# One core, hybrid attention block: the last merge gates computed as twelve seven-product groups, sums of x made earlier, norm weight folded into scales

## The chip, the core and the metric

The kernel runs on one core of a Trainium2 chip. The metric is the device time of one execution in microseconds (us). Below, PE is TensorE's matmul queue, DVE VectorE, ACT ScalarE, POOL GpSimd, and SP the queue of SyncE that issues nearly all DMAs.

## The reference

x is 2048 x 1024 (float32). What matters here:

```python
h = rms_norm(x, norm_gain[layer])
proj = h @ w_in[layer]
qa, ka, va, qb, kb, vb, ga, gb, mg = jnp.split(proj, split_idx, axis=-1)
...
br_a = ya @ w_branch_a[layer]
br_b = yb @ w_branch_b[layer]
gates = jax.nn.sigmoid(mg.reshape(bsz, S, N_BRANCHES, D) + b_merge[layer])
merged = gates[:, :, 0] * br_a + gates[:, :, 1] * br_b
x = x + merged @ w_out[layer]
```

`ya` and `yb` are the outputs of two attention mixers, each times a SiLU path. `mg` is 2048 x 2048: for each of the eight 128-wide chunks of the model dimension, a gate column block for branch 0 and one for branch 1.

## The kernel before, in words

**Precision.** Every operand of a large product is split into two float16 halves, high and low, and three products are added: high x high, high x low, low x high. x, normalised but without the norm weight, stays transposed in XH and XL (128 partitions, 8 chunks of 128 channels, 2048 tokens, and 256 wrapped around). The norm weight `gn` is multiplied into the weights on POOL (`w_gain`, line 196) before their squares are summed on ACT for a power-of-two scale (`w_square`, `w_sum`, `w_pow`), and before they are split: the high half on ACT (`w_hi`, line 249), the low half on DVE (`w_lo`, line 255). All this is done in four pieces of two channels each, 768 elements per partition for a unit.

**Units' stage.** There are 14 units of attention heads, eight slots each, 112 slots. A slot projects two blocks of 128 tokens, 2 x 24 products of 384 columns (line 710), into one of two banks called `pj`. ACT reads q and k (line 727) and the high half of v (line 736), DVE the low half of v (line 742), and only then may PE fill that bank again. Norms, transposes by DMA, logits, softmax and values of earlier blocks follow in the same slots on the other engines. Some slots carry a fill: one gate chunk for 512 tokens, 24 products of 512 columns (`FILLS`, line 115), into `pj` as well; c = 2 to 7 are chunks of the SiLU paths, c = 8 and 9 are the merge gates of chunk 6, c = 10 and 11 those of chunk 7. Chunk 3 follows after the last unit (`mg_step`). Nothing is scheduled by the compiler: every step of the other engines is pushed with a planned time in slots (`at`) and comes out between PE's products in that order (`until`), so each engine's queue is fixed by hand.

**Tail.** Then come, with times in us from its start, the merge gates of chunks 1, 5, 0, 4, 2 (`DCS`, line 46), n = 0 to 4. Tokens of q = 1 and q = 3 (quarters of 512) use `gate_pair` (line 1393), 2 x 24 products. Tokens of q = 0 and q = 2 with both branches form a 2 x 2 block product over halves of the channels, and `gate_group` (line 1490) computes it with seven block products of 12 in place of eight: four plain blocks of x, four sums of them (S1 to S4, `x_sums`, line 1436), and sums of weights (T1, T2, T3, N4, `w_sums`, line 1461). Each of the seven goes to a bank of its own and is combined on ACT, DVE and POOL. The sums of x for this token pair are made in the tail, four chains of 16 steps, and kept in the left-over part of `wt`, the tile that holds the blocks of the output weights.

```python
steps = ((whole, v1, c, 1024), (whole, v2, c + 4, 1024), (V.tensor_tensor, v2, v1, v2, OP.add), (hi, v2, 0),
```

`prep` (line 1413) loads and splits a chunk's weights, `b_load` and `b_blocks` make blocks of the output weights (j = 0 to 3, all in the tail), and some 45 tiny DVE instructions (lines 1299 to 1327) make scales at the tail's start. The tail is followed by the branch stage (`branch_pair`) and the output products (`group`), both on PE throughout.

Of the kernel before, what the change touches and what calls it, by code (L numbers as in the profile page):

```python
# [32 lines left out]
S = 2048  # L33
# [12 lines left out]
DCS = (3, 1, 5, 0, 4, 2)  # L46
# [38 lines left out]
G_LATE = {11: 0.3}  # L85
# [29 lines left out]
FILLS = ((2, None, (2, 2, 4, 5)), (3, 0, (8, 9, 10, 12)), (4, 1, (17, 18, 20, 21)), (5, 2, (24, 25, 26, 28)), (6, 3, (32, 35, 37, 38)), (7, 4, (40, 41, 42, 44)), (9, 6, (57, 59, 60, 61)), (10, 7, (64, 65, 66, 68)), (11, 10, (88, 89, 90, 92)), (8, 13, (116, 116, 118, 118)))  # L115
# [9 lines left out]
def block_kernel(tc, x, w_units, w_gate, w_mrg, w_brn, w_out, w_bra, gain, qkg, sink, bias_a, bias_b, b_merge, out):  # L125
# [15 lines left out]
    ubuf = us.tile([128, 168], F32, name="ubuf")  # L141
# [36 lines left out]
    wtiles = {}  # L178
# [17 lines left out]
    def w_gain(u, i):  # L196
        gains(wtiles[u][0], 2 * i, 384 if u < NU else 256)
# [112 lines left out]
    mgd = {k: dr.tile([128, S], F32, name=f"mgd{k}") for k in range(16)}  # L310
    ymx = us.tile([128, 32], F32, name="ymx")
# [885 lines left out]

    un, nxt = None, 0.0
# [77 lines left out]
    ygs, ypool = {}, [(fg, 6, "fg")]  # L1276
# [38 lines left out]
    V.tensor_tensor(bnd[:], invb[0][:], invb[1][:], OP.add)
    V.tensor_scalar(bnd[:], bnd[:], 2.0 ** 31, None, OP.mult)
    s_m, i_m = pow2(bnd[:], "m")

    inv_m, rmx = ucol(), ucol()
    V.tensor_tensor(inv_m[:], invb[0][:], invb[1][:], OP.max)  # L1320
    V.reciprocal(rmx[:], inv_m[:])
    for c in range(8):
        V.tensor_scalar(rho[c][:], rho[c][:], invb[c // 4][:], rmx[:], OP.mult, OP.mult)
    V.tensor_scalar(inv_m[:], inv_m[:], s_m[:], 0.125, OP.mult, OP.mult)
    i_o, so4 = ucol(), ucol()
    V.tensor_scalar(i_o[:], i_m[:], io[:], 16.0, OP.mult, OP.mult)
    V.tensor_scalar(so4[:], so[:], 0.25, None, OP.mult)
# [65 lines left out]
    def gate_pair(n, q):  # L1393
        dc, u = DCS[n + 1], NU + 1 + n
        if n not in ims:
            assert ("w", u) in done
            ims[n] = ucol()
            V.tensor_scalar(ims[n][:], wtiles[u][2][:], 0.5 / SX, None, OP.mult)
        for k in range(2):
            ps = bank()  # L1400
            g = fg.tile([128, 512], F32, name="fg", bufs=6)

            def tanh(ps=ps, g=g, k=k):
                A.activation(g[:], ps[:], AF.Tanh, bias=bmh[:, 8 * k + dc:8 * k + dc + 1], scale=ims[n][:])

            def store(g=g, k=k):
                nc.sync.dma_start(out=mgd[2 * dc + k][:, 512 * q:512 * q + 512], in_=g[:])

            e = job(5.2, tproj_list(ps, *wtiles[u][3:5], 128 * k, q))
            at(e + T_GATE[0], tanh)  # L1410
            at(e + T_GATE[4], store)

# [12 lines left out]
    def xsum(i, c):  # L1425
# [429 lines left out]
```

## Time and profile before

| | us |
|---|---|
| median of three runs | 1909.31 |
| lowest and highest run | 1909.27, 1910.56 |
| profiled execution, first to last instruction (span) | 1907.4 |
| units' stage (first to last projection) | 69.1 to 1328.7 |
| chunk 3's gates and c = 8 | 1328.7 to 1398.9 |
| tail (gates) | 1398.9 to 1593.3 |
| branch stage, output products | to 1759.2, to 1907.4 |

The page gives each engine's busy time and the chain of work that ended last; other views of the same execution give the instructions in order of time, groups of them by line and shape (count, busy time, mean of one, idle time before them and who ended it), each engine's waits, and busy time by stretch. PE's instructions are pipelined: the length shown for one is longer than the distance to the next.

### The profile page before, as it was taken

Reading aid. Unit: us, or ns where it says so; the run is one execution under the profiler, and the core shown is the slowest. Engines: PE = TensorE matmul, PEld = TensorE weight load, DVE = VectorE, ACT = ScalarE, POOL = GpSimd, SP = SyncE. Lnnn points to the kernel's source line nnn. Section 1 sums busy time; section 2 is a strip of 40 time slices with the busy share of each in tenths; the row PEclk is TensorE's granted clock in tenths of the full one; section 3 lists DMA queues with packets and bytes.
Section 4 is the critical chain, followed back from the end, with each engine's and each line's share of the span. In section 5 each row is a group of like instructions: output and inputs, shape, how many; then the busy total and the mean of one; then the engine's idle time right before and its main releaser. Section 6 shows DMA issues by size and latency. Waiting matters only on the chain.

```text
span 1907.4 us, 39286 instructions
## 1 busy us (share of the span) xinstructions
PE 1898.5 (100%) x13578; PEld 1190.9 (62%) x13578; DVE 1355.2 (71%) x3522; ACT 1119.2 (59%) x2496; POOL 848.7 (44%) x1848
## 2 busy tenths in 40 slices
PE   8999999999999999999999999999999999999999
PEld 6566776677766688566787667876544444444444
DVE  7578887887767877577776877868686667867312
ACT  8468776777666776566776767666444645423100
POOL 4334454344545655446555666555412211223443
PEclk9999999999999999999999999999999999999999
DMA  8459987798868697578768788666822246887853
GB/s 292 122 106 182 195 171 149 150 195 157 189 108 195 132 186 135 123 149 183 165 128 156 159 181 145 131 125 124 189 73 100 105 155 221 236 253 246 282 209 137
DMA packets 624585, 316.56 MB, mean 166 GB/s; under 512 B 492928, under 2 KB 562176, under 8 KB 623104
## 3 DMA queue, kind: packets, MB, share of 16 engines
q1 hardware_dynamic: 605952, 305.39, 69.3%
q10 hardware_dynamic: 18432, 8.66, 1.8%
q8 instruction: 106, 1.74, 0.4%
q14 instruction: 95, 0.78, 0.1%
HBM read 129.91 MB, written 65.27 MB: 102 GB/s over the span
## 4 chain that ended last, share of the span: by engine, by line
PE 95%; DVE 2%; POOL 1%; issue 1%; ACT 1%; DMA 0%; SPq 0%; DVEq 0%; POOLq 0%; ACTq 0%
PE pj L710 44%; PE pj L334 16%; PE fps L334 11%; PE fps L1722 6%; PE s L880 5%; PE pv L929 5%; PE fps L1517 3%; PE pj L1722 2%; PE pj L610 2%; PE pj L1517 1%; ACT jk L482 0%; DMA xt<-in_x_dram 0%; PE pt L1001 0%; DVE XL L531 0%; DVE pr L895 0%
## 5 line engine op out<-in xcount | busy, mean ns | idle before, releaser
L710 PE MATMUL pj<-wh,XL 128*128 128x384 f16 x1792 | 586.1, 327 | 0.0
L710 PE MATMUL pj<-wl,XH 128*128 128x384 f16 x1792 | 584.7, 326 | 0.0
L710 PE MATMUL pj<-wh,XH 128*128 128x384 f16 x1792 | 584.4, 326 | 0.2 <-DVE vt L742 0.2
L710 PEld LDWEIGHTS <-XH 128*128 128x128 f16 x3584 | 410.4, 116 | 151.0 <-issue 0.9
L895 DVE CUSTOM_DVE_ANT_0 pr<-s,b,ubuf 128x256 f32<-128x256 f32 (+3 forms) x512 | 219.0, 465 | 77.3 <-PE s L880 75.3
L710 PEld LDWEIGHTS <-XL 128*128 128x128 f16 x1792 | 207.8, 116 | 69.1
L912 DVE SCALAR_TENSOR_TENSOR p<-pr,p 128x512 f16<-128x512 f32 (+2 forms) x256 | 190.2, 743 | 19.1 <-ACT p L908 19.0
L787 POOL COPY spl<-spl 128x256 f16<-128x256 f16 (+1 forms) x224 | 88.6, 425 | 183.3 <-DVE spl L782 181.9
L727 ACT ACTIVATE rw<-pj 128x256 f32<-128x256 f32 (+1 forms) x224 | 86.8, 387 | 134.4 <-PE pj L710 123.2
L908 ACT ACTIVATE p<-pr 128x512 f16<-128x512 f32 (+2 forms) x256 | 159.2, 622 | 6.4 <-issue 0.3
L334 PEld LDWEIGHTS <-wh 128*128 128x128 f16 x960 | 93.7, 98 | 110.5
L880 PE MATMUL s<-kq 128*128 128x256 f16 (+3 forms) x1168 | 147.8, 254 | 0.3 <-DMA kq<-spl 0.3
L929 PEld LDWEIGHTS <-pt 128*128 128x128 f16 x3024 | 125.4, 97 | 34.8
L287 POOL TENSOR_TENSOR rs_t<-rs_y 128x8 f32<-128x8 f32 (+1 forms) x112 | 41.2, 368 | 231.3 <-DVE rs_y L279 182.7
L772 POOL TENSOR_TENSOR rw<-rw,g 128x256 f32<-128x256 f32 (+1 forms) x112 | 91.4, 816 | 109.5 <-DVE rw L766 73.1
L194 POOL TENSOR_TENSOR wraw<-wraw,gn 128x768 f32<-128x768 f32 (+1 forms) x80 | 112.5, 1412 | 56.0 <-DMA wraw<-in_w_mrg_dram 43.5
L929 PE MATMUL pv<-vt,pt 128*128 128x65 f16 (+1 forms) x3024 | 132.7, 192 | 0.0
L880 PEld LDWEIGHTS <-kq 128*128 128x128 f16 x1184 | 101.7, 98 | 42.3 <-DMA kq<-spl 0.8
L766 DVE TENSOR_TENSOR rw<-rw,qr 128x512 f32<-128x512 f32 (+1 forms) x112 | 102.6, 916 | 32.0 <-POOL qr L296 31.1
L742 DVE SCALAR_TENSOR_TENSOR vt<-pj,vt 128x128 f16<-128x128 f32 (+1 forms) x224 | 62.1, 277 | 88.6 <-ACT vt L736 87.9
L334 PE MATMUL pj<-XH,gh 128*128 128x512 f16 x320 | 121.3, 379 | 0.0
L334 PE MATMUL pj<-XH,gl 128*128 128x512 f16 x320 | 121.2, 379 | 0.0
(281 smaller groups left out, 3797.9 us busy)
## 6 DMA issues: line engine op xcount, KB each, us to landing
wraw<-in_w_units_dram SPq DMA_DIRECT2D x56, 384.0 KB, 4.4
mtd<-mm SPq DMA_DIRECT2D x56, 256.0 KB, 3.7
M<-mtd SPq DMA_DIRECT2D x8, 1792.0 KB, 9.8
mgd<-fg SPq DMA_DIRECT2D x39, 256.0 KB, 2.1
zd<-z ACTq DMA_DIRECT2D x128, 66.0 KB, 2.5
zz<-zd SPq DMA_DIRECT2D x64, 132.0 KB, 2.8
xt<-in_x_dram SPq DMA_DIRECT2D x16, 512.0 KB, 9.3
gtd<-yo SPq DMA_DIRECT2D x32, 256.0 KB, 2.9
```

What stands on the lines that cost most here:

```text
L194: G.tensor_tensor(v, v, gn[:, c0:c0 + 2].unsqueeze(2).to_broadcast([128, 2, n]), OP.mult)
L334: out.append(lambda w=w, xx=xx, ch=ch, i=i: T.matmul(ps[:], lhsT=w[:, ch, c0:c0 + 128], rhs=xx[:, ch, ts], start=(i == 0), stop=(i == n - 1)))
L710: out.append(lambda lhs=lhs, rhs=rhs, ch=ch, k=k: T.matmul(ps[:, :384], lhsT=lhs[:, ch, :], rhs=rhs[:, ch, :], start=(k == 0), stop=(k == ...
L766: V.tensor_tensor(q, q, self.rr[:, :n].unsqueeze(2).to_broadcast([128, n, HD]), OP.mult)
L772: G.tensor_tensor(k, k, GT[un.br][:].unsqueeze(1).unsqueeze(1).to_broadcast([128, 2, un.nk, HD]), OP.mult)
L787: G.tensor_copy(sp[:, i, nh:, :, :], sp[:, i, nq:nh, ::-1, :])
L880: T.matmul(self.sv[j][:, o:o + k1 - k0], lhsT=q[:, h, qo:qo + 128], rhs=kt[:, un.nq + kh + v * un.nk, k0:k1], start=(v == 0), stop=(v == 1))
L895: V.tensor_tensor_reduce(out=self.pv[:, j, self.p0:self.p0 + W], in0=self.sv[j], in1=un.bias[:, self.h0 + j, self.b0:self.b0 + W], scale=I ...
L908: A.activation(self.sp[:, :128 * n], self.pr, AF.Copy, scale=PSC)
L912: V.scalar_tensor_tensor(self.sp[:, 128 * n:], self.pr, PSC, self.sp[:, :128 * n], OP.mult, OP.subtract)
L929: T.matmul(self.po[:, j, :w], lhsT=p[:, n * j + s, :], rhs=un.v[key][:, vh, c0:c0 + w], start=(k == 0 and s == 0), stop=(k == 2 and s == n ...
L1722: mm.append(lambda ch=ch, k=k, w=w, i=i: T.matmul(ps[:, :cols.stop - cols.start], lhsT=m[:, a, ch, k, :], rhs=wt[w][:, b, ch, cols], start ...
```

## The change

- `DCS` gets chunk 7 and `NG` is 6; the fills c = 10 and 11 go, and c = 6, 9 and 7 take over slots 40 to 44, 64 to 68 and 88 to 92.
- All six chunks are computed by `gate_group` for both token pairs (p = 0: q = 0 and 2, p = 1: q = 1 and 3), the two groups of a chunk step by step in turn. `gate_pair` goes. Products whose results are only added go into the same bank without a start, three banks per group in place of seven; the additions on POOL go.
- The sums of x are made for both pairs in the units' stage, in eight chains of 16 steps spread over slots 5 to 16, 19 to 33, 44 to 59, 68 to 83 and 93 to 104, each stored to DRAM. The tail loads them back in 52 DMAs, S2 and S3 at its start.
- For units, POOL's multiplication by the norm weight goes. ACT squares each channel with the weight as its scale, and the splits use a scale per channel, so each piece is two instructions of 384.
- The tiny scale instructions move 60 us into the tail, one at a time; the output weights' blocks use the sums' scratch tile, and block j = 3 moves into the branch stage.

```diff
-DCS = (3, 1, 5, 0, 4, 2)
+DCS = (3, 1, 5, 0, 4, 2, 7)
+NG = 6
...
+X_SUM = ((5, 16), (19, 33), (44, 59), (68, 83), (93, 104)), 0.2
...
+T_R = (60.0, 1.2)
+T_X = ((1, 0.0), (2, 2.0), (0, 14.0), (3, 22.0))
...
     def w_gain(u, i):
+        if u < NU:
+            return
         gains(wtiles[u][0], 2 * i, 384 if u < NU else 256)
...
+        if u < NU:
+            for c in (2 * i, 2 * i + 1):
+                A.activation(wtiles[u][2][:, c, :], raw[:, c, :], AF.Square, scale=gn[:, c:c + 1], accum_out=wtiles[u][3][:, c:c + 1])
+            return
...
+        if u < NU:
+            wgs[u] = sm.tile([128, NCH], F32, name="gs")
+            V.tensor_scalar(wgs[u][:], gn[:], s[:], None, OP.mult)
...
+        if u < NU:
+            for c in (2 * i, 2 * i + 1):
+                V.scalar_tensor_tensor(wl[:, c, :], raw[:, c, :], wgs[u][:, c:c + 1], wh[:, c, :], OP.mult, OP.subtract)
...
+        def whole(o, ch, tok):
+            tok += 512 * p
+            V.tensor_tensor(o, XH[:, ch, tok:tok + 512], XL[:, ch, tok:tok + 512], OP.add)
+
+        def hi(v, i):
+            A.activation(sx[:, 4 + i % 3, 0], v, AF.Copy, scale=X_SC[i])
+
+        def lo(v, i):
+            V.scalar_tensor_tensor(sx[:, 4 + i % 3, 1], v, X_SC[i], sx[:, 4 + i % 3, 0], OP.mult, OP.subtract)
+            at(now[0] + X_SUM[1], store, i)
+
+        def store(i):
+            nc.sync.dma_start(out=xsd[p][:, i, c], in_=sx[:, 4 + i % 3])
...
+    times = spread(128, X_SUM[0])
+    for k in range(8):
+        x_sums(times[16 * k:16 * k + 16], k // 4, k % 4)
...
+        steps = [("x", A11, B11, one), ("y", S2, T2, lambda ps: plus("c", "a", ps)), ("x", A12, B21, two),
+                 ("y", S3, T3, lambda ps: plus("d", "a", ps)), ("z", S1, T1, done_("d", "d", 1, 2)),
+                 ("y", A22, N4, done_("a", "a", 0, 2)), ("z", S4, B22, done_("c", "c", 1, 0))]
+        if n == 0:
+            steps[1:3] = steps[2:0:-1]
+        for z, x, bl, f in steps:
+            first = z not in banks
+            if first:
+                banks[z] = bank()
+            ps = banks[z]
+            at(job(2.6, products(ps, x, bl, first)) + T_GATE[0], f, ps)
             yield
...
+    for i, d in T_X:
+        for p in range(2):
+            at(t + d + .01 * p, xs_load, p, i)
+    at(t + T_R[0], run, tail_scales())
...
-    group0 = gate_group(0)
-    for n, q in ((0, 1), (0, 3), (group0, 2), (1, 1), (1, 3), (group0, 5), (gate_group(1), 7), (2, 1), (2, 3),
-                 (gate_group(2), 7), (gate_group(3), 7), (gate_group(4), 7), (3, 1), (3, 3), (4, 1), (4, 3)):
-        if isinstance(n, int):
-            gate_pair(n, q)
-        else:
-            for _ in range(q):
-                next(n)
+    for n in range(NG):
+        for _ in zip(gate_group(n, 0), gate_group(n, 1)):
+            pass
```

## Rows read from the trace of the kernel before

**Rows 1.** The page: span, granted clock by slice, chain by engine.

```profile
span 1907.4 us, 39286 instructions
...
PEclk9999999999999999999999999999999999999999
...
PE 95%; DVE 2%; POOL 1%; issue 1%; ACT 1%; DMA 0%; SPq 0%; DVEq 0%; POOLq 0%; ACTq 0%
```

**Rows 2.** PE's waits, 69 to 1400 us: total, times, longest.

```profile
PE pj L710 <- DVE vt L742: 0.2, 1, 0.2
```

**Rows 3.** The chain in order of time, tail: start, length, count.

```profile
1445.76 7.77 PE fps L1517 x36
...
1476.87 19.64 PE fps L334 x91
```

**Rows 4.** By stretch: length; PE, PEld, DVE, ACT, POOL busy (instructions); clock; DMA share; GB/s.

```profile
129.10:280.00 150.90, 150.90 (x1440) 104.39 (x1436) 128.50 (x332) 114.37 (x248) 68.02 (x161) 1.00 0.96 179
318.20:508.80 190.60, 190.60 (x1734) 138.35 (x1733) 155.15 (x425) 140.01 (x311) 78.49 (x196) 1.00 0.85 169
640.80:786.70 145.90, 145.90 (x1182) 112.36 (x1180) 108.43 (x322) 101.56 (x255) 84.29 (x220) 1.00 0.76 154
901.60:1042.10 140.50, 140.50 (x1155) 109.94 (x1154) 105.59 (x311) 98.40 (x250) 79.25 (x214) 1.00 0.78 154
1156.20:1256.50 100.30, 100.30 (x848) 84.28 (x847) 77.38 (x242) 67.02 (x171) 55.43 (x151) 1.00 0.73 137
1016.30:1088.40 72.10, 72.10 (x593) 46.93 (x591) 57.38 (x168) 50.53 (x134) 44.80 (x118) 1.00 0.77 153
...
1398.90:1593.30 194.40, 194.37 (x905) 88.11 (x903) 132.08 (x224) 102.49 (x172) 33.32 (x26) 1.00 0.36 121
1593.30:1759.20 165.90, 165.90 (x770) 75.25 (x769) 128.31 (x188) 60.49 (x96) 43.67 (x31) 1.00 0.80 247
```

**Rows 5.** Groups by line and shape, tail: the sums' steps today.

```profile
L1449 DVE SCALAR_TENSOR_TENSOR wt<-Y,wt 128x512 f16<-128x512 f32 x16 | 11.8, 736 | 0.1
L1445 ACT ACTIVATE wt<-Y 128x512 f16<-128x512 f32 x16 | 10.1, 629 | 15.3 <-DVE Y L434 15.1
```

**Rows 6.** Groups by line and shape: splits of 768 (units), of 384 (tail).

```profile
L259 DVE SCALAR_TENSOR_TENSOR wl<-wraw,ubuf,wh 128x768 f16<-128x768 f32 x53 | 56.9, 1073 | 9.9 <-ACT wh L253 9.0
L253 ACT ACTIVATE wh<-wraw,ubuf 128x768 f16<-128x768 f32 x52 | 48.1, 925 | 0.0
L1381 DVE SCALAR_TENSOR_TENSOR wl<-wraw,ubuf,wh 128x384 f16<-128x384 f32 x8 | 4.8, 614 | 4.0 <-ACT wh L1380 4.0
L1380 ACT ACTIVATE wh<-wraw,ubuf 128x384 f16<-128x384 f32 x8 | 4.4, 602 | 0.0
```

**Rows 7.** L766: min/median/max ns, then its group; in order of time, one collision.

```profile
L766 DVE TENSOR_TENSOR rw<-rw,qr x112: 678/693/2071, 83.0 to 1338.1; 128x512 f32<-128x512 f32 x96, 128x640 f32<-128x640 f32 x16
...
L766 DVE TENSOR_TENSOR rw<-rw,qr 128x512 f32<-128x512 f32 x95 | 84.7, 892 | 28.9 <-POOL qr L296 28.1
...
298.01 2.07 DVE L766 TENSOR_TENSOR rw<-rw,qr 128x640 f32<-128x640 f32 x1 [0.94 <-POOL qr L296]
...
297.93 1.47 POOL L194 TENSOR_TENSOR wraw<-wraw,gn 128x768 f32<-128x768 f32 x1
```

**Rows 8.** PE in order of time at one refilled bank: start, length.

```profile
1093.02 0.32 PE L710 MATMUL pj<-wh,XH 128*128 128x384 f16 x1 [0.23 <-DVE vt L742]
```

**Rows 9.** DVE in order of time: the first unit's last low half.

```profile
68.66 1.01 DVE L259 SCALAR_TENSOR_TENSOR wl<-wraw,ubuf,wh 128x768 f16<-128x768 f32 x1
```

**Rows 10.** DMA: throughput by slice, landing of a store, SP's issues around the tail's start.

```profile
GB/s 292 122 106 182 195 171 149 150 195 157 189 108 195 132 186 135 123 149 183 165 128 156 159 181 145 131 125 124 189 73 100 105 155 221 236 253 246 282 209 137
...
mgd<-fg SPq DMA_DIRECT2D x39, 256.0 KB, 2.1
...
1394.62 5.53 SPq L417 DMA_DIRECT2D mgd<-yo  x2
1404.76 1.41 SPq L189 DMA_DIRECT2D wraw<-in_w_mrg_dram  x3
```

More of the change, by code (lines that the diff above doesn't have):

```diff
@@ L310, in block_kernel @@
     mgd = {k: dr.tile([128, S], F32, name=f"mgd{k}") for k in range(16)}
+    xsd = [dr.tile([128, 4, 4, 2, 512], F16, name=f"xsd{p}") for p in range(2)]
+    sx = us.tile([128, 7, 2, 512], F16, name="sx")
     ymx = us.tile([128, 32], F32, name="ymx")
@@ L1315, in block_kernel @@
[L1315 to L1325, printed above, removed]
@@ L1334, in block_kernel, with run @@
+    def run(steps):
+        if next(steps, run) is not run:
+            at(now[0] + T_R[1], run, steps)
     A11, A12, A22, S1, S2, S3, S4 = range(7)
@@ L1391, in block_kernel @@
     ims = {}
[L1393 to L1411, printed above, removed]
     def prep(t, u):
@@ L1517, in products @@
                     mm.append(lambda ch=ch, k=k, w=w, i=i: T.matmul(
-                        ps[:], lhsT=weight(bl, ch)[w], rhs=xblock(x, ch)[k], start=(i == 0), stop=(i == 11)))
+                        ps[:], lhsT=weight(bl, ch)[w], rhs=xblock(x, ch, p)[k], start=(first and i == 0), stop=(i == 11), skip_group_check=not first))
             return mm
-        def copy(o, ps, scale):
-            A.activation(o, whole(ps), AF.Copy, scale=scale)
-        def plus(o, ps, v, scale):
-            V.scalar_tensor_tensor(o, whole(ps), scale, v, OP.mult, OP.add)
@@ L1527, in add @@
-        def add(o, x, y):
-            G.tensor_tensor(o, x, y, OP.add)
-        def gate(o, v, k, q, late):
-            at(now[0] + late, lambda: A.activation(o, v, AF.Tanh, bias=bmh[:, 8 * k + dc:8 * k + dc + 1], scale=ims[n][:]))
-            at(now[0] + late + T_S[6], lambda: nc.sync.dma_start(out=whole(mgd[2 * dc + k][:, 512 * q:512 * q + 512]), in_=o))
-        def two(ps):
-            d = tile_()
-            plus(d, ps, a, 1.0)
-            gate(d, d, 0, 0, T_S[8])
-        steps = ((A11, B11, lambda ps: copy(a, ps, 1.0)), (A12, B21, two), (S1, T1, lambda ps: copy(b, ps, 16.0)),
-                 (S2, T2, lambda ps: (plus(c, ps, a, 16.0), add(a, b, c))),
-                 (S3, T3, lambda ps: (plus(c, ps, c, 16.0), add(b, b, c), gate(b, b, 1, 2, T_S[7]))),
-                 (S4, B22, lambda ps: (plus(a, ps, a, 4.0), gate(a, a, 1, 0, T_S[8]))),
-                 (A22, N4, lambda ps: (plus(c, ps, c, 4.0), gate(c, c, 0, 2, T_S[8]))))
@@ L1544, in gate_group, with gate @@
-        for k, (x, bl, f) in enumerate(steps):
-            if k == 0 and n:
-                a = tile_()
-            if k == 2:
-                b, c = tile_(), tile_()
-            ps = bank()
-            at(job(2.6, products(ps, x, bl)) + T_GATE[0], f, ps)
-            yield
-    t = clock[0]
+        def gate(o, v, k, q, late, first=False):
+            at(now[0] + late, lambda: A.activation(o, v, AF.Tanh, bias=bmh[:, 8 * k + dc:8 * k + dc + 1], scale=ims[n][0 if first else 1][:]))
+            at(now[0] + late + T_S[6], lambda: nc.sync.dma_start(out=mgd[2 * dc + k][:, 512 * (q + p):512 * (q + p) + 512], in_=o))
@@ new lines, in gate_group, with one, plus, done_ @@
+        v = {}
+        def one(ps):
+            v["a"] = tile_("a")
+            A.activation(v["a"], ps[:], AF.Copy, scale=0.0625)
+        def two(ps):
+            gate(tile_("d"), ps[:], 0, 0, 0, True)
+        def plus(o, w, ps):
+            if o not in v:
+                v[o] = tile_(o)
+            V.tensor_tensor(v[o], ps[:], v[w], OP.add)
+        def done_(o, w, k, q):
+            def f(ps):
+                plus(o, w, ps)
+                gate(v[o], v[o], k, q, T_S[8])
+            return f
@@ L1554, in block_kernel @@
+    t = t0 = clock[0]
+    s2 = [y0.tile([128, 2, 4, 512], F16, name=f"Y0{p}") for p in range(2)]
+    for i, d in T_X:
+        for p in range(2):
+            at(t + d + .01 * p, xs_load, p, i)
+    at(t + T_R[0], run, tail_scales())
     for n, b, d in T_P:
```

205 lines of the change are left out of this document (122 added, 83 removed).

## The prediction

> **What bounds the kernel now.** I read the page first: TensorE (PE) runs at full granted clock throughout, and 95% of the chain that ended last is PE [rows 1]. A busy PE proves little, so I next asked who PE waited for. Over the whole stretch from the first unit into the tail, DVE kept it waiting 0.2 us, once, for the low half of v (L742) [rows 2]. Then the chain in order of time: in the tail the products stand back to back, 36 in 7.77 us and 91 in 19.64 us [rows 3], which is 0.2158 us for a product of 512 columns whatever its line. So this kernel is a PE queue without holes. A product removed is worth 0.2158 us, unless another engine fails to keep up; a product moved is worth nothing. The rest of the reading is therefore about the spare time of the others, above all VectorE (DVE), stretch by stretch [rows 4].
>
> **The products.** Removed from the units' stage: the fills c = 10 and 11 (chunk 7), 2 x 4 x 24 = 192 products. In the tail, the five chunks now take 5 x 2 x 2 x 24 = 480 plain ones (tokens of q = 1 and 3) and 5 x 7 x 12 = 420 in groups. Afterwards there are twelve groups of 7 x 12, 1008. So 192 + 480 + 420 - 1008 = 84 fewer: 84 x 0.2158 = **18.1 us**. By stage: the units lose 41.4 us, the tail grows from 194.2 to 217.5 us.
>
> **The sums of x, in the units.** Eight chains of 12 DVE and 4 ScalarE (ACT) instructions and 4 stores replace four chains in the tail. DVE: 96 x 0.736 = 70.7 us; ACT: 32 x 0.629 = 20.1 us [rows 5]. The 32 stores join SP's queue behind their own low half, planned 0.2 of a slot earlier, 0.47 us of SP each [rows 10], 15 us in 66 slots; the transposes queued behind them would be late only if DVE were late by more than that. Nothing here is on PE's path as long as DVE has room. In the five stretches where the change puts the steps, DVE stands idle 22.4, 35.4, 37.5, 34.9 and 22.9 us [rows 4], 153 in all, or about 143 once two of the removed fills shorten them.
>
> **Norm weight folded.** POOL loses its 56 multiplications of unit weights, of 1.47 us and the like [rows 7]. In exchange each 768-wide square, high and low instruction becomes two of 384. DVE: 2 x 0.614 - 1.073 = 0.155 us, x 56 = 8.7 us; ACT: 2 x 0.602 - 0.925 = 0.279 us, for squares and highs, x 112 = 31 us [rows 6]. ACT idles over 200 us in the five stretches [rows 4], so it covers this; without that cover it would cost up to those 51 us. DVE also gets something back: its multiplication L766 takes 0.693 us in the median but 2.07 us at worst (a 640-wide one), started while POOL multiplies a weight [rows 7]. The mean of 0.892 over 95 of them is 19 us above the median in total, part of which goes.
>
> The row shows this collision as a doubling or worse of one DVE instruction. The Trainium skill (SBUF — State Buffer, Who interferes with whom) states it as a rule: a DVE instruction with two SBUF inputs and a GpSimd instruction that reads SBUF exclude each other, and the second waits in full. The trace agrees on the size: 2.07 us is near 0.69 + 1.47. The rule speaks for the fold, and against the sums, all of whose DVE steps have two SBUF inputs; by it alone the time would lie nearer the first of the rivals below.
>
> As bounds for DVE: from below 70.7 + 8.7 - 19 = 60 us; from above each sum step costs the 0.892 of L766 [rows 7], 85.6 + 8.7 = 94 us. I take 77, nearer the tail's rows, which are the same instructions. 77 fits into 143 idle, on average. The first stretch is the tightest: 11 of 66 slots, 16 steps, 11.8 us plus about 1 against 22.4, which lifts DVE from 85% to about 94%.
>
> **Where that can reach PE.** Projection banks come in two; PE may refill one only when ACT and DVE have read it. I paired each L742 with PE's next write of its bank over the units: the spare is 3.2 us in the median of 222, under 1.0 us in 12 and nil in three, one of which is the wait of [rows 8]. Six of the 12 lie in the five stretches, with 0.20, 0.81, 0.05, 0.66, 0.17 and 0.63 us. If one added instruction of about 0.6 us (0.736 less what neighbours overlap) stands ahead at each, PE loses 0.4 + 0.55 + 0.43 = 1.4 us; if two do, 4.7 us. Nil if the relief cancels it. Steps are half a slot apart, so one is likelier: I take **+1.6 us**.
>
> Two B0 units lose their fills and get the load of the two later units that never had any; the one at 1016 us runs without a wait at 80% DVE [rows 4], so I cost that at nothing.
>
> **The start.** The first unit's last low half ends at 69.67 us [rows 9], the first pair starts at 69.1 and reaches that chunk 12 products of 0.163 us later, at 71.1. Four low halves split in two cost 0.6 us of the 1.4 us of spare: nil, at most 0.5 us.
>
> **The tail's start.** x's sums now come from DRAM. SP is held until 1400.15, 1.2 us into the tail, by the last gate's store [rows 10]; then come 2 MB of S2 and 2 MB of S3 in 20 issues, 9.4 us of SP. At 292 GB/s, the best slice, and 2.1 us as a store takes to land [rows 10], S2 of the first half lands 6.9 us in and is wanted at 10.4; the whole 4 MB at 17.7, wanted at 18.1. At 246 GB/s, a slice of the branch stage, it would be 20.4, a loss of 2.3 us. Between nil and 2.3 I take **+0.4 us**: the later half alone is close. The tail's 45 tiny scale instructions leave DVE's start there, so the weights' sums begin some 5 us sooner. S1 and S4 have more room. Behind the 20 issues SP has the next chunk's weights, wanted 36 us in, and the first gate stores, which nobody waits for before their tile comes round again.
>
> **In the tail** a bank is added into again only after its reader: 7.8 us later, in the first group 2.6 us, against a copy of 0.6 us: nil. DVE is busy 132 of 194 us there [rows 4], and loses four chains of 12 (35 us) and one output block (about 8 us) while it gains 35 additions of 0.69 and one more chunk's weights (10 us). The output block moves to the next stage, where DVE has 37 us idle [rows 4] and PE has eight banks of 2.6 us each: nil.
>
> **Sum.** -18.1 + 1.6 + 0.4 = -16.1. The profiled execution spans 1907.4 us and the median of the runs is 1909.3, so about 1.9 us lie around the span and stay. 1909.3 - 16.1 = **1893.2 us**.
>
> **Rivals.**
> - *DVE short of room in the units.* For it: 94% in the first stretch, and idle time before a wait is not all usable. Against: no wait now. If 45% of the 153 us is usable, 77 - 69 = 8 us are lost: 1899. Chance 0.18.
> - *The sums come late.* The tail's first group waits 2 to 6 us for S2 or S3, as 4 MB of 1 KB rows share the queues with gate stores: 1893 to 1897. Chance 0.08.
> - *Slower: DVE becomes the bound in the units.* In place: the five stretches. If a third of the idle time is usable, 77 - 51 = 26 us are lost, 1917. It decides from 38% usable down, where the loss passes 18.1. POOL's chain of ten small instructions, which DVE waits for, being blocked by the new steps would lead there. Against: all L766 together wait 28.1 us for POOL today [rows 7], in 14 units. Chance 0.06.
> - *The saving is not there*, because accumulated banks do make PE wait: 12 groups revisit four banks each, 48 x about 0.4 us gives it all back: 1909. The interleaving of two groups speaks against it. Chance 0.04.
> - My forecast, PE still without holes: 0.64, with its own range 1890 to 1896.
>
> **Range and chances.** 1890 (no new wait, 0.7 us of old ones gone) to 1902 takes in the forecast, the late sums and most of the first rival; what is left out is the slower ones and some of the tail. About 0.2% (3.8 us) is what a measurement can tell from no change. Faster needs less than 1905.5: 0.64 + 0.08 + 0.17 = 0.89; within 0.2%: 0.05; slower 0.06.
>
> **What would show it.** Right: the tail from its first product to the branch stage is 217.5 us, the units end about 41 us earlier, PE's waits in the units sum to under 3 us and name L742 or the copy of q and k. Wrong: PE waiting for S2 or S3 in the first 20 us of the tail; DVE above 95% in slots 5 to 16 with PE holes there; product spacing in the tail above 0.2158; or a group's products waiting for tanh or for an addition on their own bank.

## The result, and the profile after

The changed kernel takes 1913.46 us (median of 13 runs, 1911.3 to 1916.64) against 1909.55 us (13 runs) of the kernel before: a ratio of 1.0022, interval 1.0015 to 1.003. It is slower by 3.9 us, where the forecast was 16.1 us faster. The profiled execution of the changed kernel took 1916.64 us, 3.2 us above its median; its span is 1914.8 us.

The page of the changed kernel, its answers to [rows 1]: span, busy time of each engine, granted clock by slice, chain by engine.

```profile
span 1914.8 us, 39519 instructions
...
PE 1887.6 (99%) x13493; PEld 1183.4 (62%) x13493; DVE 1388.3 (73%) x3691; ACT 1157.5 (60%) x2692; POOL 760.3 (40%) x1782
...
PEclk9999999999999999999999999999999999999999
...
PE 8%; DMA 4%; DVE 2%; issue 1%; ACT 1%; POOL 0%; SPq 0%; DVEq 0%; ACTq 0%; POOLq 0%
```

PE is still busy 99% of the time, and every slice still shows a 9 for the clock. The chain looks as if PE's 95% [rows 1] had become 8%, but its shares add up to 16% of the span: it is followed back only to about 1590 us. So it says nothing of the units and the tail, and of what comes after them only that DMA, DVE and ACT stand in the chain beside PE. A chain that leaves PE shows that PE waited somewhere. How much, and where, needs the stages. These are the windows of the changed kernel, cut at PE's first product of each stage and at the end of the last projection (columns as in [rows 4]: length; PE, PEld, DVE, ACT, POOL busy; clock; DMA share; GB/s):

```profile
0.00:70.30 70.30, 64.21 (x409) 41.44 (x410) 54.11 (x157) 55.46 (x108) 19.48 (x20) 1.00 0.77 234
70.30:1297.90 1227.60, 1220.84 (x10166) 865.43 (x10166) 994.91 (x2895) 883.68 (x2215) 588.66 (x1619) 1.00 0.80 163
...
1368.10:1594.20 226.10, 220.44 (x1014) 99.29 (x1013) 124.53 (x260) 106.49 (x177) 22.82 (x20) 0.98 0.45 148
1594.20:1766.10 171.90, 167.21 (x769) 75.00 (x768) 127.44 (x187) 62.10 (x99) 41.96 (x30) 1.00 0.78 242
```

Beside the stages of before (cut in the same way from its trace) and what the removed products alone would give, at 0.2158 us each:

| stage, us | before | products alone | after | given back |
|---|---|---|---|---|
| start | 69.1 | 69.1 | 70.3 | 1.2 |
| units | 1259.6 | 1218.2 | 1227.6 | 9.4 |
| rest of chunk 3, chunk 8 | 70.0 | 70.0 | 70.2 | 0.2 |
| tail | 194.5 | 217.8 | 226.1 | 8.3 |
| branch | 165.8 | 165.8 | 171.9 | 6.1 |
| output | 148.4 | 148.4 | 148.6 | 0.2 |
| span | 1907.4 | 1889.3 | 1914.8 | 25.5 |

So in this execution the 18.1 us came and 25.5 us were given back, nearly all in three places. By the medians 18.1 + 3.9 = 22.0 us were given back; the profiled execution is slower than its median. PE's waits in the changed kernel name a different producer in each (us in total, times, longest):

```profile
PE fps L1563 <- DMA wt<-xsd: 4.6, 1, 4.6
PE pj L735 <- DVE vt L767: 3.8, 6, 1.6
PE s L905 <- DMA kq<-spl: 3.4, 3, 2.5
PE fps L359 <- DVE kp L1708: 2.4, 3, 1.8
PE fps L359 <- DVE fg L1708: 1.4, 2, 1.0
...
PE fps L219 <- ACT wl L247: 1.0, 1, 1.0
PE fps L359 <- DVE Y L1353: 0.9, 2, 0.5
```

Before, the units had only the wait of 0.2 us in [rows 2]. The stretch of [rows 2] has one more wait that those rows leave out, behind the units, at 1350 us:

```profile
PE s L880 <- DMA kq<-spl: 0.3, 1, 0.3
```

**Units** (L735, L767 and L905 were L710, L742 and L880 before). The six waits for vt fall into the stretches of the sums or, in one case, just behind one, where the prediction looked for them, but last up to 1.6 us. The wait for kq had been priced at nothing. Around it, the changed kernel's timelines of DVE, ACT and SP (start, length, instruction, idle time before it and its releaser):

```profile
656.19 1.22 DVE L1235 SCALAR_TENSOR_TENSOR sx<-sx 128x512 f16<-128x512 f32 x1
657.90 0.75 DVE L1049 SCALAR_TENSOR_TENSOR yo<-yh,ubuf,yo 128x512 f32<-128x512 f32 x1 [0.49 <-ACT yh L1043]
...
656.50 1.37 ACT L1043 ACTIVATE yh<-ya 128x1024 uint16<-128x1024 uint16 x1 [1.67 <-DMA ya<-yh]
...
659.69 0.43 SPq L1239 DMA_DIRECT2D xsd<-sx  x1
660.42 3.30 SPq L820 DMA_TRANSPOSE kq<-spl  x2
```

A sum's low half takes 1.22 us (0.69 in the median), and its store stands on SP just ahead of the two transposes of q and k, whose issues take 3.30 us. They land 6.8 and 5.3 us after they were issued; the same two took 3.7 and 3.4 us in the kernel before. PE stands still from 664.8 to 667.3 us and then runs for 3.4 us at half clock: the window from 667.4 to 671.0 us has a granted clock of 0.56, which costs 3.6 x 0.44 = 1.6 us. The waits for vt (3.8), those for kq in this stage (2.9) and the clock (1.6) make up 8.3 of the 9.4 us.

**Tail.** The wait of 4.6 us is for S1, not for S2 or S3. SP's issues at the start of the tail, in order of time (start, time on the queue, count):

```profile
1369.60 2.10 SPq L1494 DMA_DIRECT2D Y<-xsd  x4
1371.92 10.24 SPq L1498 DMA_DIRECT2D wt<-xsd  x12
1382.48 1.74 SPq L1498 DMA_DIRECT2D sx<-xsd  x4
1384.32 1.92 SPq L195 DMA_DIRECT2D wraw<-in_w_mrg_dram  x4
1386.34 0.89 SPq L1569 DMA_DIRECT2D mgd<-fd  x2
1387.27 6.77 SPq L1498 DMA_DIRECT2D wt<-xsd  x9
```

Twelve loads of S3 hold SP for 10.24 us, 0.85 each, where the four after them take 0.43 each. Most of these issues are themselves no longer than that: the last row below has their length in ns (least, median, most). But between them SP waits for earlier loads to land, as its waits from 1369 to 1394 us show (us in total, times, longest):

```profile
SPq L1498 <- DMA Y<-xsd: 3.0, 3, 1.2
SPq L1498 <- DMA wraw<-in_w_mrg_dram: 1.5, 3, 0.7
...
L1498 SPq DMA_DIRECT2D wt<-xsd x26: 319/430/1218, 1371.9 to 1396.0; - x26
```

S1 is issued from 1387.27 us, 1.6 us before PE wants it, and its first load takes 6.3 us to land. And in short windows of the changed kernel:

```profile
1376.00:1380.00 4.00, 4.00 (x20) 1.76 (x19) 0.75 (x1) 1.66 (x3) 0.00 (x0) 1.00 1.09 351
1380.00:1384.00 4.00, 4.00 (x20) 1.86 (x19) 0.82 (x2) 0.00 (x0) 0.00 (x0) 1.00 0.75 223
1384.00:1388.00 4.00, 4.00 (x21) 1.77 (x19) 0.56 (x1) 0.00 (x0) 0.19 (x1) 1.00 0.79 240
1388.00:1393.50 5.50, 1.01 (x5) 0.38 (x4) 0.78 (x2) 2.17 (x6) 3.72 (x4) 0.81 0.91 300
1393.50:1398.00 4.50, 4.36 (x12) 1.61 (x12) 0.80 (x3) 0.72 (x2) 0.17 (x1) 0.50 0.87 280
```

The last row is PE at half clock behind the wait: 12 products in 4.5 us, a loss of 4.5 x 0.50 = 2.2 us. The DMA engines are at work all the time, at 351, 223, 240 and 300 GB/s. With the 1.0 us before a sum of squares (L219) wait and clock make 7.8 of the 8.3 us.

**Branch.** PE's banks are held by gate products (L1708), and these stand on DVE between merge blocks (mm) and the block of w_out that the change put there (wt, wraw). DVE in order of time, and then PE's row:

```profile
1685.79 0.74 DVE L1416 SCALAR_TENSOR_TENSOR wt<-wraw,ubuf,wt 128x512 f16<-128x512 f32 x1
1686.45 1.76 DVE L1416 SCALAR_TENSOR_TENSOR mm<-kp,ubuf,mm 128x512 f16<-128x512 f32 x1
1688.14 0.74 DVE L1353 SCALAR_TENSOR_TENSOR Y<-yq,ubuf,Y 128x512 f16<-128x512 f32 x1
1688.80 0.74 DVE L1416 SCALAR_TENSOR_TENSOR wt<-wraw,ubuf,wt 128x512 f16<-128x512 f32 x1
1689.46 0.68 DVE L1437 TENSOR_TENSOR wraw<-wraw 128x512 f32<-128x512 f32 x1
1690.06 0.68 DVE L1708 SCALAR_TENSOR_TENSOR kp<-kp,fps 128x512 f32<-128x512 f32 x1
...
1690.79 0.59 PE L359 MATMUL fps<-Y,wh 128*128 128x512 f16 x2 [1.79 <-DVE kp L1708]
```

### The profile page after: what moved, and what is told of

Read it like the earlier page. It is cut to its first block, busy times and chain, and to the rows that moved or that the text cites. A ratio compares the mean times of both kernels' runs of the same rounds, so it can differ in the third digit from the quotient of the medians.

```text
span 1914.8 us, 39519 instructions
## 1 busy us (share of the span) xinstructions
PE 1887.6 (99%) x13493; PEld 1183.4 (62%) x13493; DVE 1388.3 (73%) x3691; ACT 1157.5 (60%) x2692; POOL 760.3 (40%) x1782
## 5 line engine op out<-in xcount | busy, mean ns | idle before, releaser
L735 PE MATMUL pj<-wh,XH 128*128 128x384 f16 x1792 | 585.0, 326 | 4.5 <-DVE vt L767 3.8
L735 PE MATMUL pj<-wh,XL 128*128 128x384 f16 x1792 | 586.8, 327 | 0.0
L735 PE MATMUL pj<-wl,XH 128*128 128x384 f16 x1792 | 585.4, 327 | 0.0
L735 PEld LDWEIGHTS <-XH 128*128 128x128 f16 x3584 | 411.4, 116 | 156.2 <-issue 7.6
L735 PEld LDWEIGHTS <-XL 128*128 128x128 f16 x1792 | 207.7, 116 | 67.8 <-issue 0.5
L905 PE MATMUL s<-kq 128*128 128x256 f16 (+3 forms) x1168 | 147.8, 254 | 3.4 <-DMA kq<-spl 3.4
L905 PEld LDWEIGHTS <-kq 128*128 128x128 f16 x1184 | 101.6, 98 | 44.9 <-DMA kq<-spl 4.7
L1715 POOL TENSOR_TENSOR kp<-kp,fg 128x512 f32<-128x512 f32 x32 | 45.3, 1419 | 203.5 <-DVE fg L1708 123.1
L791 DVE TENSOR_TENSOR rw<-rw,qr 128x512 f32<-128x512 f32 (+1 forms) x112 | 87.0, 777 | 45.9 <-POOL qr L319 45.3
L928 ACT ACTIVATE pr<-pr,z 128x128 f32<-128x128 f32 (+2 forms) x256 | 98.8, 438 | 35.3 <-DVE z L920 35.1
L359 PE MATMUL fps<-Y,wh 128*128 128x512 f16 x384 | 114.5, 379 | 4.7 <-DVE kp L1708 2.4
L1774 PEld LDWEIGHTS <-M 128*128 128x128 f16 x684 | 66.9, 98 | 78.4
L359 PEld LDWEIGHTS <-wh 128*128 128x128 f16 x640 | 62.2, 98 | 78.0 <-issue 4.3
```

The source lines that it names most:

```text
L359: out.append(lambda w=w, xx=xx, ch=ch, i=i: T.matmul(ps[:], lhsT=w[:, ch, c0:c0 + 128], rhs=xx[:, ch, ts], start=(i == 0), stop=(i == n - 1)))
L735: out.append(lambda lhs=lhs, rhs=rhs, ch=ch, k=k: T.matmul(ps[:, :384], lhsT=lhs[:, ch, :], rhs=rhs[:, ch, :], start=(k == 0), stop=(k == ...
L791: V.tensor_tensor(q, q, self.rr[:, :n].unsqueeze(2).to_broadcast([128, n, HD]), OP.mult)
L905: T.matmul(self.sv[j][:, o:o + k1 - k0], lhsT=q[:, h, qo:qo + 128], rhs=kt[:, un.nq + kh + v * un.nk, k0:k1], start=(v == 0), stop=(v == 1))
L928: A.activation(v, v, AF.Exp, bias=self.stat(j), scale=-1.0)
L1774: mm.append(lambda ch=ch, k=k, w=w, i=i: T.matmul(ps[:, :cols.stop - cols.start], lhsT=m[:, a, ch, k, :], rhs=wt[w][:, b, ch, cols], start ...
```

## The experiments

All are edits of the changed kernel. Times are medians, ratios are against the kernel before, stage lengths come from one profiled execution each. Where the code of a stage is untouched its length still varies: units 1224.8 to 1228.3 us (seven kernels), branch 169.3 to 171.9 us (seven kernels). Smaller differences than that are not read, and the branch stage's loss of 6.1 us is the upper end of 3.5 to 6.1 us.

**e1_no_sums.** Sixteen steps of each chain are left out, the stores stay, and what they store is a constant.

```diff
-        for k, (f, *args) in enumerate(steps):
-            at(ts[k], f, *args)
+        for k, i in ((6, 0), (11, 2), (13, 1), (15, 3)):
+            at(ts[k] + X_SUM[1], store, i)
```

> Left out: all 128 DVE and ACT steps that make the sums of x in the units; the 32 stores and 52 loads stay and carry a constant. Theory (the sums crowd DVE and ACT in the units): the units' stage goes from 1227.6 us to 1218 to 1220, the length that 192 fewer products alone give (1259.6 - 41.4 = 1218.2), and the total falls by 8 to 10 us; tail (226) and branch stage (172) keep their lengths. Rival (the fold's smaller instructions do it): the units stay at 1225 or more and the total moves by under 3 us.

Measured: 1906.18 us, ratio 0.998 (0.997 to 0.9989); units 1219.9 us; the time fell by 7.3 us, a little less than the expected 8 to 10. PE's waits:

```profile
PE fps L1564 <- DMA wt<-xsd: 3.4, 1, 3.4
PE s L906 <- DMA kq<-spl: 1.8, 1, 1.8
```

All waits for vt are gone, and no stretch of the units is at half clock. The steps on ACT and DVE cost 7.7 of the 9.4 us (4.9 to 8.4 against the seven kernels); the stores alone don't. The other 1.7 us is a wait for kq at 662 us, which the kernel before does not have. The steps do not make it, but the stores, which this run keeps, are not ruled out: in the kernels that have a store right ahead of these transposes this wait is 1.3 to 2.7 us, in the five where the store was moved away (f1, f4, g3, h1, i1) it is between none and 1.4 us.

**e2_no_fold.** The norm weight is multiplied by POOL again, and squares and splits of the units' weights are 768 wide.

```diff
-        if u < NU:
-            for c in (2 * i, 2 * i + 1):
-                V.scalar_tensor_tensor(wl[:, c, :], raw[:, c, :], wgs[u][:, c:c + 1], wh[:, c, :], OP.mult, OP.subtract)
-        else:
...
+        c = slice(2 * i, 2 * i + 2)
+        V.scalar_tensor_tensor(wl[:, c, :n], raw[:, c, :n], s[:], wh[:, c, :n], OP.mult, OP.subtract)
```

> The norm weight is multiplied on POOL again and the units' weights are squared and split in pieces of 768, as before; the rest is the change. Rival (the fold's smaller instructions crowd ACT and DVE): the units' stage falls from 1227.6 us to about 1219 and the start by 1 us. Theory (the sums do it, the fold helps): the units' stage is no shorter, 1227 to 1240, since DVE again waits behind POOL's weight multiplications; the total is 1913 to 1926.

Measured: 1922.93 us, ratio 1.0064 (1.0047 to 1.0081); units 1236.4 us. A wait of PE:

```profile
PE pj L718 <- DVE vt L750: 11.2, 13, 2.4
```

And on its page the group of the multiplication that was L766 (busy, mean ns, idle before):

```profile
L774 DVE TENSOR_TENSOR rw<-rw,qr 128x512 f32<-128x512 f32 (+1 forms) x112 | 105.5, 942 | 71.5 <-POOL qr L302 71.2
```

The fold is worth 8.8 us in the units. The same group has a mean of 916 ns in the kernel before and 777 ns after, 112 x 0.139 = 15.6 us of DVE. The Trainium skill (SBUF — State Buffer, Who interferes with whom) says that such a DVE instruction, with two inputs in SBUF, and a GpSimd instruction that reads SBUF exclude each other; these means agree. The start may be the one place where the fold costs: it takes 69.7 us here, without the 0.6-us wait (L735 for L438) that the changed kernel has in front of its first pair. But the same start takes 69.8 to 70.4 us in the thirteen kernels with the fold, and f1, at 70.4 us, does not have that wait either.

**e3_no_block3.** The last quarter of w_out is not loaded or split.

```diff
-    at(t + T_OB[0], b_load, 3)
-    at(t + T_OB[1], b_blocks, t + T_OB[1], 3)
+    done.update(("b", 3, b) for b in range(7))
```

> Left out: loading and making block j = 3 of the output weights in the branch stage (4 loads, 7 highs, 7 lows, 4 differences). Theory (this moved work makes the branch stage's waits): the branch stage falls from 171.9 us to 165.8 to 167, the total by 5 to 6 us. Rival (the waits come from the end of the tail, whose late steps now run into the branch stage): it stays at 170 or more.

Measured: 1910.43 us, ratio 1.0001 (0.9992 to 1.0011); branch 166.6 us. The waits for L1708 are gone, so the "nil" of the branch stage was wrong, by 5.3 us against the changed kernel's profile and by 2.7 to 5.3 us against the seven kernels. The time fell by 3.0 us, less than the 5 to 6 us expected. Its trace also shows where DVE does have room, two gate products in order of time:

```profile
1707.30 0.69 DVE L1708 SCALAR_TENSOR_TENSOR fg<-fg,fps 128x512 f32<-128x512 f32 x1
1716.21 0.69 DVE L1708 SCALAR_TENSOR_TENSOR kp<-kp,fps 128x512 f32<-128x512 f32 x1 [8.23 <-DMA kp<-mgd]
```

The trace of the kernel before has the same wait, and it could have been read there:

```profile
1715.56 0.69 DVE L1658 SCALAR_TENSOR_TENSOR kp<-kp,fps 128x512 f32<-128x512 f32 x1 [8.94 <-DMA kp<-mgd]
```

**e4_s1_early.** `T_X`'s entry (0, 14.0) becomes (0, 2.1): S1 is issued ahead of the next chunk's weights.

> The loads of S1 are issued directly behind those of S3, ahead of the next chunk's weights and the first gate stores; nothing else. Theory (S1 waits for its place in SP's queue): PE's wait of 4.6 us and the half clock after it go, the tail falls from 226.1 us to 218 to 221, the total by 5 to 8. Rival (the tail's first 36 us want more bytes than the DMA engines move): the wait moves to the weights, in the sum of their squares or in the next chunk's first product, and the tail stays at 223 or more.

Measured: 1920.14 us, ratio 1.0052 (1.0037 to 1.0067); tail 232.0 us. The largest wait of PE:

```profile
PE fps L219 <- ACT wl L247: 12.3, 2, 11.3
```

The wait for sums is gone and one for the weights' sum of squares has its place. So order alone was not the fault: what was put behind S1 came late instead. That fits too many bytes for the time, which f2 and g2 test.

**f1_windows.** The sums' steps are moved, none is taken away.

```diff
-X_SUM = ((5, 16), (19, 33), (44, 59), (68, 83), (93, 104)), 0.2
+X_SUM = ((5, 13.5), (18, 29.5), (33, 36), (41, 44.8), (49, 60), (65, 68.8), (73, 84), (89, 92.8), (96, 105.5)), 0.2
```

> Edit: the sums' 128 steps keep their number and their order and are moved into stretches of the units' stage in which VectorE stands idle in the run without the sums (slots 5 to 13.5, 18 to 29.5, 33 to 36, 41 to 44.8, 49 to 60, 65 to 68.8, 73 to 84, 89 to 92.8, 96 to 105.5). Theory (a step costs only where its slot has no room on VectorE): the units' stage falls from 1227.6 us to 1220 to 1222 (1219.9 without the sums), the waits of pj matmuls for vt together under 1 us (3.8 in the changed kernel), and the time from 1913.5 to 1906 to 1909. Rival (the sums cost the same wherever they stand, by the collision with POOL and by SP's stores): the stage stays at 1226 to 1229 and the time at 1912 to 1915.

Measured: 1910.53 us, ratio 1.0005 (0.9996 to 1.0014); units 1222.1 us, the wait for kq 0.9 us, no half clock in the units; the waits for vt only fell to 2.6 us (3.8 after), where the theory had under 1. The stage is 0.1 us above the theory's range; the time lies 1.5 us above its range, probably because that counted from a profiled run above its median.

**f2_s2_early.** One megabyte less in the tail's first loads.

```diff
+    at(107.0, lambda: nc.sync.dma_start(out=sx[:, :4], in_=xsd[0][:, 1]))
...
-    s2 = [y0.tile([128, 2, 4, 512], F16, name=f"Y0{p}") for p in range(2)]
+    bscr = y0.tile([128, 4, 512], F32, name="Y00")
+    s2 = [sx[:, :4], y0.tile([128, 4, 2, 512], F16, name="Y01")]
```

> Edit: the S2 sums of the lower 512 tokens are loaded into the sums' scratch with one DMA at slot 107, ahead of the tail, and S2 of the upper tokens with one DMA (1 MB, 8-KB rows); the blocks of w_out that used that scratch in the tail get another. Theory (the tail's first 36 us want more bytes than the DMA engines bring): 1 MB less is 2.9 to 4.5 us at the 351 to 223 GB/s that the windows there show, so the wait for S1 (4.6 us) and the stretch at half clock after it (6.8 us long, cost 3.4) go, the tail falls from 226.1 us to 218 to 220, and the time from 1913.5 to 1905 to 1908. Rival (the wait only moves to the weights or to S4, as it did when S1 was loaded ahead of the weights): the tail stays at 224 to 228 and the time at 1911 to 1916.

Measured: 1911.59 us, ratio 1.0009 (0.9999 to 1.0018); tail 222.6 us, in neither range; the time is in the rival's. The wait for S1 is 1.6 us instead of 4.6, two more of 0.9 together follow, and no half clock. The wait shrank with the bytes, as the theory says, and the step was too small. (The expectation's 3.4 us for the half clock counted all 6.8 us of it; PE ran in 4.5 of them, 2.2 us.)

**f3_spread.** The seven splits of the branch stage stand 6.3 us apart instead of 1.55.

> Edit: the seven block splits of w_out's last quarter in the branch stage stand 6.3 us apart instead of 1.55. Theory (they cost as a burst, each step in front of a gate's product on VectorE): the branch stage falls from 171.9 us to 166 to 167.5 (166.6 without these steps), the time from 1913.5 to 1908 to 1910.5. Rival (VectorE has no room for them in that stage however they stand): 169.5 to 172 and 1911.5 to 1914.

Measured: 1915.64 us, ratio 1.0027 (1.0017 to 1.0037); branch 169.9 us, inside what untouched code gives. The theory of the burst falls: spread out, the splits cost as much.

**f4_all.** The three edits together.

> Edit: the three edits of this call together (sums in roomy slots, S2 of the lower tokens early, the last quarter's splits spread). Theory (three separate causes that add): units 1220 to 1222, tail 218 to 220, branch 166 to 167.5, the time 1895 to 1900, and so under the 1909.6 of the kernel before and near the forecast of 1893.2. Rival (the three share one cause, the profile's lower clock or VectorE's total): less than 10 us of gain, 1903 to 1910.

Measured: 1906.72 us, ratio 0.9983 (0.9974 to 0.9992); units 1222.8, tail 223.6, branch 169.5 us. Faster than both kernels, but the time lies in the rival's range, not in the theory's: the tail and the branch stage are as short of the expectation as in f2 and f3.

**g1_block_late.** `T_OB` from (58.0, 66.0) to (100.0, 115.0).

> Edit: the last quarter of w_out is loaded and split in one burst as before, 49 us later in the branch stage (its splits from 115 us into the stage instead of 66), behind the merge blocks. In the run without these splits VectorE is idle there for 10.7 of the 15.6 us from 114.4 to 130.0 us into the stage, and for 0.0 to 2.9 us in each 5.2 us of the place where they stand now. The eleven instructions want about 8 us. Theory (place, not spacing: they cost only beside the merge blocks): the branch stage falls from 171.9 us (169.3 to 172 in the runs that have them) to 166 to 167.5, and the time to 1908 to 1911. Rival (their mere number costs, wherever they stand): 169 to 172 and 1911.5 to 1915.

Measured: 1916.2 us, ratio 1.0034 (1.0022 to 1.0046); branch 171.8 us. The edit did not do what it was meant to do. ACT's first split:

```profile
1722.19 0.72 ACT L1415 ACTIVATE wt<-wraw,ubuf 128x512 f16<-128x512 f32 x1 [15.77 <-DMA wraw<-in_w_out_dram]
```

The load stood on SP behind gate loads until 1712.5 us, so ACT stood 15.8 us waiting for it and the splits came 13 us late, on top of the next merge blocks. This says nothing on place against number.

**g2_early_all.** As f2, with 768 KB more loaded at slot 107 (the pieces in `sx[:, 4:7]`).

> Edit: as the run with S2 of the lower tokens loaded early, and the three other pieces that lie in the sums' own tile (768 KB) are loaded at slot 107 too. Theory (bytes before the first S1 product set the wait): 0.75 MB less in the tail's first 25 us is another 2.2 to 3.4 us at 351 to 223 GB/s, so the waits for sums that were left (1.76, 0.49 and 0.74 us) go, and the tail falls from 222.6 us to 218.5 to 220.5 (217.6 and the 1.1-us wait at the sum of squares); the time is 1906 to 1910. Rival (the rate falls with the bytes, since SP issues the 128-KB loads one by one behind what has landed): waits of 2 us or more stay, the tail 222 to 224, the time as with S2 alone, 1911.6.

Measured: 1908.32 us, ratio 0.9993 (0.9984 to 1.0003); tail 219.5 us. No wait for a sum is left; the one before L219 (1.0 us) is the largest in the tail. In all 1.75 MB less turned 226.1 into 222.6 and 219.5 us: the bytes ahead of the first S1 product set that wait. Both edits also took issues from SP, but SP was itself waiting for loads to land.

**g3_best.** g2's early loads, now at slot 110.5, g1's late block, and three shifts in tables.

```diff
-X_SUM = ((5, 16), (19, 33), (44, 59), (68, 83), (93, 104)), 0.2
+X_SUM = ((5, 13.5), (18, 28), (33, 35), (42, 44.5), (49, 60), (66, 68.5), (73, 84), (90, 92.3), (97, 109.5)), 0.2
-T_P = ((0, 0.0, 0.03), (1, 7.0, 31.0), (2, 37.5, 60.5), (3, 69.4, 92.4), (4, 105.8, 128.8), (5, 142.2, 165.2))
+T_P = ((0, 0.0, 0.03), (1, 7.0, 31.0), (2, 37.5, 60.5), (3, 70.8, 92.6), (4, 105.8, 128.8), (5, 142.2, 165.2))
-T_R = (60.0, 1.2)
+T_R = (46.0, 1.2)
```

> Edit: the early loads and the late last quarter of this call, the sums' steps once more moved out of slots in which a wait was left (28 to 29.5, 41, 65, 89, 96), and in the tail the chain of scales 14 us earlier and the fourth chunk's preparation 1.4 us later (for the 1.1-us wait at its sum of squares). Theory (each wait has its own cause, and they add): units 1220.5 to 1223, tail 217.5 to 219.5, branch 166 to 167.5, the time 1898 to 1902, inside the forecast's range at its upper end. Rival (a wait removed makes another one late): 1904 or more, no better than the three edits of the last call (1906.7).

Measured: 1902.16 us, ratio 0.996 (0.9947 to 0.9972), 0.2 us above the range. Units 1219.5 and tail 218.4 us; the branch stage is still 171.5 us, not 166 to 167.5.

**h1_best_gap.** g3 with the load back at 58 and the splits, 0.55 us apart, from 109.6. With this spacing the program takes the high half of the last block before its subtraction, and the low half, made after it, carries the rest.

> Edit: as the last combined kernel, but the last quarter of w_out is loaded at 58 us into the branch stage, as in the changed kernel (the later load stood behind the gates' loads in SP's queue and landed 9 us after it left), and its eleven splits and subtractions are put, 0.55 us apart, in front of the pair of gate products for which VectorE stood still 8.2 us, waiting for a load of gates (at 1708 us in the run without the splits). Theory (place: they cost nothing where VectorE waits for a DMA): the branch stage falls from 171.5 us to 166.5 to 168.5 (two waits of 0.5 and 0.6 us at its start have another cause), the time from 1902.2 to 1897 to 1900. Rival (VectorE makes up in that gap what the merge blocks before it left behind, so eleven steps more come late anywhere): 169.5 to 172 and 1900.5 to 1903.

Measured: 1901.0 us, ratio 0.995 (0.9938 to 0.9963); branch 171.0 us, the rival's figures. But the program's order had not done what was meant. DVE in order of time:

```profile
1702.09 0.74 DVE L1423 SCALAR_TENSOR_TENSOR wt<-wraw,ubuf,wt 128x512 f16<-128x512 f32 x1
1707.91 0.69 DVE L1721 SCALAR_TENSOR_TENSOR kp<-kp,fps 128x512 f32<-128x512 f32 x1 [5.08 <-DMA kp<-mgd]
1708.52 0.75 DVE L1423 SCALAR_TENSOR_TENSOR wt<-wraw,ubuf,wt 128x512 f16<-128x512 f32 x1
```

The third split ends before the gap, a product that waits for its gates comes fourth, and four splits run behind it. DVE stood still for 5.08 us with work behind the waiting instruction.

**i1_best_gap2.** The same place, all splits ahead of that product.

```diff
-            at(t0 + T_B[2] * i, hi)
-            at(t0 + T_B[2] * i + T_B[3], lambda lo=lo, b=b: (lo(), done.add(("b", j, b))))
+            d, e = (.33 * i, .1) if j == 3 else (T_B[2] * i, T_B[3])
+            at(t0 + d, hi)
+            at(t0 + d + e, lambda lo=lo, b=b: (lo(), done.add(("b", j, b))))
```

> Edit: as the last kernel, but all eighteen instructions of the last quarter's splits stand in the order of the programs between the two pairs of gate products around the gap; in the last kernel only three of the seven low halves did, a product that waited 5.1 us for its gates came fourth, and the other four ran after it, among the merge blocks. Theory (place): the branch stage falls from 171.0 us to 166.5 to 168.5, the time from 1901.0 to 1896.5 to 1899. Rival (number: VectorE has no room for them anywhere in this stage, since what runs in the gap delays the merge blocks behind it): 170 to 172 and 1900 to 1902.5.

Measured: 1897.13 us, ratio 0.994 (0.9927 to 0.9954). Its windows by stage (columns as above):

```profile
0.00:70.10 70.10, 63.53 (x410) 41.12 (x411) 54.22 (x157) 55.75 (x108) 18.96 (x20) 1.00 0.77 235
70.10:1290.10 1220.00, 1218.27 (x10166) 865.26 (x10166) 995.86 (x2891) 884.83 (x2214) 592.45 (x1617) 1.00 0.81 165
...
1360.00:1578.50 218.50, 218.24 (x1015) 98.69 (x1014) 126.25 (x260) 106.31 (x178) 22.98 (x20) 1.00 0.44 145
1578.50:1745.40 166.90, 166.18 (x769) 75.10 (x768) 127.98 (x187) 61.73 (x99) 41.91 (x30) 1.00 0.79 249
```

Place, not number: the branch stage is 166.9 us with the same splits. Every engine does the work of the changed kernel (DVE 995.86 us in the units against 994.91), in a span of 1894.0 us in place of 1914.8. This version is 0.6% faster than the kernel before and 16.3 us faster than the changed one.

## Why the prediction was wrong, point by point

- **The products, -18.1 us: right.** 192 products fewer in the units (-41.4) and 108 more in the tail (+23.3). The table's last column is not products; most of it is accounted for by waits and clock.
- **The work, right; its place, wrong.** The prediction put DVE's added sums at 77 us (bounds 60 to 94, the folds within). The sums alone take 71.2 us in the changed kernel (96 instructions, mean 0.742). The folds cost 13.0 us, not 8.7 (112 low halves of 0.690 us in place of 56 of 1.069), and give back 15.6 us at L766's successor, 68.6 us in all. The first step that failed is "Steps are half a slot apart, so one is likelier: I take +1.6 us". It measured 9.4 us. Of this the sums' steps make 7.7 (e1), mostly by where they stand: moved, the same steps leave 1222.1 and 1222.8 us (f1, f4) and, moved once more, 1219.5 to 1221.5 us (g3, h1, i1), 1.3 to 3.3 above the products alone. So +1.6 is near what well-placed sums cost. The bound of 4.7 looked only at the banks of the projections, and the waits for vt, 3.8 us, stayed within it. Outside it were the transposes of q and k, which the prediction named and priced at nothing (2.9 us of wait in the units), and PE's clock after that wait (1.6 us). By its own sign the units were to end about 41 us earlier, with under 3 us of waits; they ended 30.8 us earlier, with 6.7.
- **The start, nil and at most 0.5: wrong**, 1.2 us (0.7 to 1.3 in the kernels with the same start). A wait of 0.6 us stands at the first pair and is gone without the fold (e2), but also in f1, whose start is no shorter. The cause is not shown.
- **The tail's start, +0.4: mis-sized, 8.3 us.** The prediction worked out S2 and S3 against the queue, which held up. The second step that failed is "S1 and S4 have more room", written without a sum. Up to S1's first load SP issues S2, S3, the next chunk's weights, two gate stores and that load, 5.6 MB. By the prediction's own rates (SP free 1.2 us in, 292 GB/s, 2.1 us to land) it is there 23.5 us in; S1 is wanted 20.8 us in. The load landed 25.5 us in. e4, f2 and g2 show bytes, not order. The half clock (2.2 us) and the wait before L219 (1.0 us, behind an output block and the scale chain; gone in g3, which moved two things at once) came with it.
- **The block in the branch stage, nil: wrong**, 6.1 us here and 3.5 to 6.1 in the seven kernels. This is the third step that failed. The cover named was "DVE has 37 us idle". That is a sum over the stage: 8.9 us of it is one wait for a load, and beside the merge blocks there was not enough. e3 and i1 show both halves.
- **The rivals.** The first, DVE short of room in the units, had the size of the units' loss (8 us) but not the reason: the room sufficed in i1. The second, sums late by 2 to 6 us, was the tail's event with S1 in place of S3, and got 0.08. None was for the branch stage, and none for several of them at once; the slower rival, DVE as the bound, did not happen.

What stays open: the cause of the 1.8-us wait for kq that e1 keeps (0.5 us or less in g3 and i1, 1.3 in h1), and the start's 1.2 us.

## What to carry to other kernels

Idle time summed over a stage covers nothing by itself: ask what the instruction lands in front of, and read the queue behind it, since the same 128 steps left the units 9.4 us (the changed kernel), 3.9 us (f1) or 1.8 us (i1) above their products by their slots. For a stage that begins with loads, add up all bytes that are due, in order of their due times, and not only the first. Before work is hidden in a gap, look whose wait the gap is, and put all of it ahead of the instruction that waits.

## What was not expected of the hardware

- PE's granted clock fell to half in or right after some waits: for 3.4 us after 2.5 us of wait in the units, for 6.8 us around the 4.6-us wait in the tail (row 1393.5 to 1398: 0.50), and for 10.2 us in and after the 11.3 us of e4. In e1 no such stretch followed the wait of 1.8 us. What counts is the part in which PE runs: it lost 1.6 us, 2.2 us and, with 3.6 us of work at a clock of 0.51, 1.8 us in e4, whose wait was by far the longest. The Trainium skill (TensorE: Matmul & The Clock Gate, Part 1) knows the two levels, 1.2 and 2.4 GHz; the rows of 1.00 and 0.50 agree.
- Of the 128-KB loads at the tail's start the first twelve held SP's queue for 0.85 us each and the nine of S1 for 0.75, while the DMA engines moved 223 to 351 GB/s. The issue itself was 0.43 us in the median, near the prediction's 0.47 us. A few took up to 1.22 us, and SP stood still between issues until earlier loads had landed, 3.0 us for S2 and 1.5 us for the weights. So SP's time there cannot be had from a price per issue alone.
